# Rotating the order of nine projection units so that two accumulators stay open, with side work placed anew and 32 groups of seven products instead of 33

## The chip, the cores and the metric

The kernel runs on one core of a Trainium2 chip. The metric is the time of the whole program on the device in microseconds (us). TensorE is called PE in the profile, VectorE DVE, ScalarE ACT, GpSimd POOL, and SyncE SP; SP only issues transfers here. Three runs of the kernel before gave 1335.2, 1333.42 and 1333.69 us, with a median of 1333.69 us.

## The reference, cut to what matters

One layer of a diffusion backbone is applied to two groups of 128 tokens (a prompt and a latent grid), model width D = 2048, all in fp32:

```python
sh1, sc1, g1, sh2, sc2, g2 = split(silu(cond) @ w_ada + b_ada)   # per group, w_ada 2048 x 12288
h = rms_norm(x, norm1_w) * (1 + sc1) + sh1
qa, ka, va, qb, kb, vb, ga, gb = split(h @ w_in)                  # w_in 2048 x 8704
oa, ob = window_attention(qa, ka, va), neighbourhood_attention(qb, kb, vb)
x = x + g1 * ((sigmoid(ga) * (oa @ w_br_a) + sigmoid(gb) * (ob @ w_br_b)) @ w_out)
h2 = rms_norm(x, norm2_w) * (1 + sc2) + sh2
x = x + g2 * (square(relu(h2 @ w_up)) @ w_down)                   # 2048 x 8192, 8192 x 2048
```

The outputs are x for both groups and the new keys and values. With only 256 rows of activations, the work is a stream of weights: every weight is read once.

## The kernel before, in words

**Steps.** The weights stream through as 456 steps of one 128x1024 fp32 tile (512 KB, tile `raw`). To keep fp32 accuracy with fp32r products, each tile is split in two: ACT copies it to `wH` (line 93, the helper `copy`), DVE subtracts to get `wL` (line 241), and PE makes three products for each pair of operands: high by high, high by low, low by high. A plain step is 12 matmuls of 128x128 by 128x512. Steps 0 to 71 are the first part (q, k and v of the input projection), 72 to 135 the gates, 136 to 199 the merge and the output projection, 200 to 215 the first eighth of `w_up`. Then `up` and `down` alternate: 16 steps of `w_up` for the next eighth (`up_pair`, L1113), 16 steps of `w_down` for the one before (`down_unit`, L1252), seven times, and 16 steps of `w_down` at the end. Pair 6 is steps 376 to 391, pair 7 steps 408 to 423; behind each come four units of `w_down`, steps 392 to 407 and 424 to 439.

**The first part.** Nine units of 512 columns (`first_units`, L367) are done in five chunks of the inner dimension (`CHUNKS`, 2, 2, 2, 4 and 6 tiles of 128 rows), because the modulation of the rows (`mod_pair`, L415, from pairs of `w_ada` tiles called `araw`, L300, multiplied at L308) is made while it goes on. `start_steps` (L379) runs one unit over one chunk. Each unit has two accumulators of one PSUM bank each; the pool `pacc` has four banks, so two units can be open. At the end of its chunk, a unit is either held open (`hold`, L399) or its two banks are read out: the first time by ACT copies (L403, `first_evac`), afterwards by two DVE adds to the unit's sum in SBUF (L406). Before, the order of units is reversed from chunk to chunk (L433), so the last unit of one chunk is the first of the next, and that one is held.

**Groups of seven.** In `up_pair`, the eight positions of a pair are either plain (two steps, 24 matmuls) or a group of seven products (a step x and a step y, 21 matmuls together, by a recombination of 2x2 blocks). `FAST` lists which positions are groups. A group saves three matmuls, but it needs more of the others: on ACT the copies `XH`, `YB` (half a tile), `tH` and `uH`, on DVE the sum `t` (L1178), three half-tile operations (L1181 to L1183) and the differences `XL`, `tL` and `uL` (L1186 to L1188). `prep_x` issues `XH`; `prep_y` issues all the rest as one block, in the order of the code. A pair opens four banks of `pacc`, Q1, Q6, Q2 and Q7 (L1137), and four of another pool. At position 0 the y step multiplies Q2 first, then Q7, then Q6 (L1123 to L1125).

**The end of a unit of w_down.** `down_unit` adds its two banks to `dsum` on DVE (L1263), except for the units in `SUM_DMA`, where two ACT copies move the banks into a `dsum` part, which a POOL transfer with addition (L1267) adds later. Unit 23 (the fourth unit after pair 6, steps 404 to 407) is one of those.

**Order of the work.** `run` (L264) writes out the program step by step; every engine then works through its own list in that order. For step i it issues loads up to the due time i + `RUN[i]`, then splits (the `prep` functions) up to step i + `LOOK[i]`, then the matmuls of step i with their end, then side work due at i. `LO_DMA` lists steps whose `wL` is made by an ACT pass with sign and a POOL transfer with addition (L247, L248) in place of the DVE operation. All 128x1024 tiles, weights and their halves among them, come from one pool of 48 slots (`GEN`), so a load can wait for a slot. SP issues loads in a single list, in the order written. `DOTS1`, `DOTS`, `DOTS2`, `SS_AT`, `JOBS`, `POST` and the like are due steps of side work (other parts of `w_ada`, attention).

Of the kernel before, what the change touches and what calls it, by code (L numbers as in the profile page):

```python
# [32 lines left out]
FB_DVE = 6  # L33
FB1 = 14
H_AT = 41
DOTS1 = [11, 17, 20, 28, 28, 31, 34, 37]
CHUNKS = [2, 2, 2, 4, 6]
NFAST = 8
FAST = {1: (0, 3, 7), 2: (0, 2, 6, 7), 3: (0, 2, 4, 5, 7), 4: (0, 2, 4, 5, 7), 5: (0, 3, 4, 5, 7), 6: (0, 2, 4, 5, 7), 7: (0, 1, 2, 4, 5, 7)}
SUM_DMA = [5, 6, 11, 13, 16, 19, 21, 23, 25, 27]  # L40
AWAY = [('gA', 1), ('gB', 2), ('gB', 3), ('gA', 0), ('gB', 0), ('gA', 2)]
GATE_BACK = 8
DIRECT = (3,)
LO_DMA = [70, 83, 107, 131, 176, 184, 233, 292, 314, 328, 402, 404]
LO_AHEAD = 2

LOOK = "443323444122344433223333332123333453344534333554455544344534333543324554444555556665556644444333333333332222122312344544555434333333342344333334333323445566643344456656533344434444445455564546555553444554322355444554433333333434334533333333333654544332334455543444555653215536544523333334543233333332223323365455455443222212233432443334434642333334444544534434333333333325434222223333434444444434555642255353443444442222432331122132223342112223332233345544"
RUN = "301110000000010212223333322222222221111122244455544355434445554334554445555664543433234334444445665543321222222212444444444444442222222232223344444455544544444444555455454445566644455555554543365434343355445756644443566664333312222234552332223333334545332333333333322211122222332233322212233323323332332112344444442343322211333343334323233334544422742222212223445554422333233322222211222333333435767545333110221112232111233456655566567556433435335553333334"
CONST_AT = [65, 67]
XL_DMA = []  # L50
ADA_AT = [None, 4, 13, 18, 21, 36, 29]
XS_AT = {1: 13, 2: 18, 3: 29}
POST = {('kvA', 0): [67, 70, 75], ('qA', 0): [70, 73, 78], ('qA', 1): [72, 74, 80], ('kB', 0): [77, 83, 90], ('qB', 0): [82, 84, 93], ('kB', 1): [86, 91, 93], ('qB', 1): [90, 93, 97]}
JOBS = [[79, 80, 80, 87, 93], [81, 83, 88, 90, 93], [87, 87, 89, 90, 99], [93, 93, 96, 99, 102], [96, 97, 100, 105, 112], [102, 103, 107, 112, 123], [105, 107, 111, 118, 123], [112, 115, 118, 121, 123]]
SS_AT = [43, 51, 73, 75, 139, 139]
T_AT = [4, 4]
PREP_IN = [6, 7]
DOTS = [33, 39, 42, 43, 47, 47, 48, 49, 52, 54, 55, 57, 60, 62, 69, 70, 73, 77, 80, 84, 90, 91, 92, 92, 94, 98, 101, 103, 103, 105, 108, 110, 111, 112, 115, 118, 120, 121, 122, 122, 126, 127, 128, 129, 130, 132, 132, 136, 137, 138, 138, 143, 144, 147, 147, 150, 153, 155, 157, 161, 164, 167, 170, 172, 173, 174, 175, 176, 177, 178, 179, 182]
DOTS2 = [230, 232, 234, 235, 236, 237, 240, 243, 255, 263, 265, 269, 270, 288, 301, 301, 307, 328, 328, 331, 333, 334, 358, 360, 361, 363, 366, 368, 391, 391, 395, 399]
STAT_AT = [-1, 0, 10, 16]  # L60
T_PAIR = [[8, 9], [6, 8], [8, 9], [7, 8], [10, 11], [8, 9], [12, 11]]
P_PAIR = [[4, 2], [2, 4], [3, 4], [1, 3], [6, 6], [3, 3], [6, 5]]
M_TE = (3,)
M_AT = [1, 3, 9]
FLIP = 1
P_UP = [4, 1]
T_UP = [6, 5]
COL = {"qA": 0, "kvA": 1024, "qB": 1536, "kB": 2560, "vB": 3584, "gA": 4608, "gB": 6656}


# [1 line left out]
def tile_hybrid_step(ctx: ExitStack, tc: tile.TileContext, a):  # L72
# [188 lines left out]

    by_dma = sorted(LO_DMA)

    def run():  # L264
        loads.sort(key=lambda x: x[:2])
        for st in wsteps:
            while loads and loads[0][0] <= st["i"] + int(RUN[st["i"]]):
                loads.pop(0)[2]()
            for j in sorted(j for j in pre if j <= st["i"]):
                for fn in pre.pop(j):  # L270
                    fn()
            to = st["i"] + int(LOOK[st["i"]]) + 1
            while by_dma and by_dma[0] < to + LO_AHEAD:
# [93 lines left out]
    first_units = [("qA", 0), ("qA", 1), ("kvA", 0), ("qB", 0), ("qB", 1), ("kB", 0), ("kB", 1), ("vB", 0), ("vB", 1)]  # L367
    late_units = []
    nf = len(first_units)
# [9 lines left out]
    def start_steps(u, k0, nk, held, hold):  # L379


        box = {}

        def mm(st, kt):
            if kt == 0:
                box["acc"] = open_acc.pop(u) if held else [bank("acc", pacc) for _ in range(2)]
            acc = box["acc"]
            wh, wl = st["hl"]
            last = kt + 2 == nk
            for k in range(2):  # L390
                g, kg = divmod(k0 + kt + k, 4)
                for tb in range(2):
                    sh, sl = hH[g][:, kg, tb, :], hL[g][:, kg, tb, :]
                    pe.matmul(acc[tb], sh, wh[:, k, :], start=kt == 0 and k == 0 and not held, stop=False)  # L394
                    pe.matmul(acc[tb], sh, wl[:, k, :], start=False, stop=False)  # L395
                    pe.matmul(acc[tb], sl, wh[:, k, :], start=False, stop=last and k == 1 and not hold)  # L396
            if not last:
                return
            if hold:  # L399
                open_acc[u] = acc  # L400
                return
            if u not in units:
                first_evac(u, acc)  # L403
                return
            for tb in range(2):
                dve.tensor_tensor(units[u][:, tb, :], units[u][:, tb, :], acc[tb], op=OP.add)  # L406
            box.clear()

        for kt in range(0, nk, 2):
            add_step(wsrc(w_in, k0 + kt, COL[u[0]] + 512 * u[1]), lambda st, kt=kt: mm(st, kt), u)  # L410
# [4 lines left out]
    def mod_pair(f):  # L415

        box, k0 = {}, 2 * f
        i = ADA_AT[f]
        for j in range(2):
# [9 lines left out]
    for g, i in XS_AT.items():  # L429
        at(i, lambda g=g: x_scale(g))  # L430
    k0 = 0
    for c, nk in enumerate(CHUNKS):
        for j, u in enumerate(first_units[::-1] if c % 2 else first_units):  # L433
            start_steps(u, k0, nk, c > 0 and j == 0, c < len(CHUNKS) - 1 and j == nf - 1)
        k0 += nk

    def begin():
# [108 lines left out]
    def unit_gate(u):  # L546
        def evac(acc):
            gates[u] = G(f"g_{u[0]}{u[1]}").rearrange("p (s n) -> p s n", s=2)
            for tb in range(2):
                act.activation(gates[u][:, tb, :], acc[tb], AF.Sigmoid if u in direct else AF.Copy)  # L550
            if u in AWAY:
                gate_mem[u] = dp.tile([P, 1024], F32, name=f"gm_{u[0]}{u[1]}")
# [62 lines left out]
    s0 = len([st for st in wsteps if st["key"] in first_units])  # L615
    load_at(CONST_AT[0], load_consts)
    load_at(CONST_AT[1], load_bias)

# [58 lines left out]

    for u, ps in POST.items():
        nh = 2 if u[0] == "kvA" else 4
# [99 lines left out]
    att_end = 0  # L779
    for (mix, s, g), js in zip([("A", 0, 0), ("A", 1, 0), ("A", 0, 1), ("A", 1, 1), ("B", 0, 0), ("B", 1, 0), ("B", 0, 1), ("B", 1, 1)], JOBS):  # L780
        need = [POST["kvA", 0][2] + 1, POST["qA", g][2] + 1] if mix == "A" else [
            POST["kB", g][2] + 1, POST["qB", g][2] + 1, end_of(("vB", g)) + 1]
        assert js[0] >= max(need) and list(js) == sorted(js)
# [8 lines left out]
    def sigmoids():  # L792
        for u in gates:
            if u not in direct and u not in AWAY:
                sigmoid(u)
# [93 lines left out]
    for n in range(4):  # L889
        br_unit(n)  # L890
    for u in AWAY:
        i = end_of(("y" + u[0][1].lower(), u[1]))
        load_at(i - GATE_BACK, lambda u=u: gate_back(u))
        at(i - 2, lambda u=u: sigmoid(u))
# [81 lines left out]
    def norm2(s):  # L976
# [3 lines left out]
        rsqrt(r, ms, EPS)  # L980
        prep_to(end_of(("out", 3)) + 1 + PREP_IN[s])
        for n in range(4):
# [130 lines left out]
    def up_pair(p):  # L1113
        n0, n1 = PIECES[p]
        w, box, key = a["w_up"], {"begun": set()}, ("up", n0)
        fast = FAST[p]

# [134 lines left out]
    def down_unit(p, n):  # L1252
        def evac(acc):
            by_pool = 4 * p + n in SUM_DMA
            if p == 0 or by_pool:
# [24 lines left out]
    for n in range(4):  # L1280
        at(end_of(("up", 0)) + 1 + n, lambda n=n: x1_away(n))
    for g in range((max(len(f) for f in FAST.values()) + 1) // 2):
        at(end_of(("up", 0)) + STAT_AT[g], lambda g=g: fast_stat(g))
    for p in range(len(PIECES)):
        if p < last and p + 1 not in FAST:
            for n in PIECES[p + 1]:
# [92 lines left out]
    jobs1 = [((0, w), fb) for fb in range(FB1, KC) for w in range(2)]  # L1379
    first = list(zip(DOTS1, [(j, 0, 0) for j in jobs1] + [(j, 1, 1) for j in jobs1], strict=True))  # L1380
    placed = list(zip(DOTS, [(j, 1, 0) for j in g1 + ss] + [(j, 0, 1) for j in g1 + ss], strict=True))
    assert DOTS[-1] < end_of(("out", 2))
# [12 lines left out]
    for c in range(FB_DVE // 2):  # L1395
        box = {}
        for j in range(2):
            i = SS_AT[2 * c + j]
            load_at(i, lambda box=box, c=c, j=j: pair_load(box, 1, 2 * c + j))
# [104 lines left out]
```

## The time and the profile before, and how to read them

| | |
|---|---|
| median of three runs | 1333.69 us (1333.42 to 1335.2) |
| the profiled execution's own time | 1333.2 us |
| its span | 1331.4 us, mean granted TensorE clock 0.998 |
| traffic | 392.24 MB, mean 295 GB/s |

The profiled execution's time is 1.8 us above its span, for what lies around the span. All positions in time are counted in us from the span's start. The profile gives each engine's busy time, windows of time with each engine's busy time and instruction counts, groups of like instructions with the mean time of one, the waits of an engine with what ended them, the timeline of single instructions, and a chain of waits followed back from the last instruction. In a window, the number in brackets behind a busy time counts the instructions that lie in it, also in part; PEclk is the clock granted to TensorE as a share of full speed. Matmuls are pipelined: one shows some 390 ns, but the next one starts earlier, so it is the distance from start to start that tells PE's pace.

### The profile page before, as it was taken

To read this page: it belongs to the slowest core of one execution; us is meant where nothing else is said; L and a number is where in the kernel's file an instruction comes from. 1 tells how busy PE (TensorE), PEld (TensorE's weight loads), DVE (VectorE), ACT (ScalarE), POOL (GpSimd) and SP (SyncE) were. 2 spreads that over 40 slices of the span, in tenths; PEclk is the share of its full clock that TensorE was granted. 3 is DMA by queue.
4 is the path that set the end of the run, shared out by engine and by line. 5 is a ranking of instruction groups with operands and counts; after the bars stand their busy time and mean duration, and the time that the engine had idled before them with its cause. 6 is when DMAs were issued, how large, how long until landed. Compare 5 with 4: busy or idle time off the path is not lost.

```text
span 1331.4 us, 18029 instructions
## 1 busy us (share of the span) xinstructions
PE 1316.4 (99%) x6411; PEld 1067.2 (80%) x6412; DVE 1185.6 (89%) x1538; ACT 801.2 (60%) x979; POOL 54.0 (4%) x64
## 2 busy tenths in 40 slices
PE   8999999999999999999999999999999999999998
PEld 4777778788888878888888888888888888877887
DVE  4589999988898999999779998998999999989685
ACT  5534443476656446635677866758576576676670
POOL 0000000521000000000000000000000000000000
PEclk9999999999999999999999999999999999999999
DMA  9999998987589999996577876988797696988962
GB/s 372 408 409 408 409 398 303 383 277 240 182 326 354 383 394 352 362 359 218 191 225 279 285 252 214 290 278 264 237 298 252 237 300 206 313 192 296 329 210 98
DMA packets 148266, 392.24 MB, mean 295 GB/s; under 512 B 51792, under 2 KB 53008, under 8 KB 148176
## 3 DMA queue, kind: packets, MB, share of 16 engines
q1 hardware_dynamic: 144448, 378.16, 78.9%
q0 software_dynamic: 3584, 12.85, 5.0%
q8 instruction: 50, 0.82, 0.2%
q14 instruction: 40, 0.33, 0.1%
q10 hardware_dynamic: 144, 0.08, 0.0%
HBM read 367.16 MB, written 8.68 MB: 282 GB/s over the span
## 4 chain that ended last, share of the span: by engine, by line
PE 93%; DMA 4%; ACT 1%; DVE 1%; issue 0%; SPq 0%; DVEq 0%; ACTq 0%
PE acc L291 17%; PE acc L292 17%; PE acc L293 17%; PE Q L1123 6%; PE Q L1124 6%; PE Q L1125 6%; PE acc L394 4%; PE acc L395 4%; PE acc L396 4%; DMA araw<-in_w_pair 3%; PE ps_ada L308 2%; PE ps_S L713 1%; PE Z L1124 1%; PE Z L1123 1%; PE Z L1125 1%; DMA aT<-in_w_adaT 1%
## 5 line engine op out<-in xcount | busy, mean ns | idle before, releaser
L241 DVE TENSOR_TENSOR wL<-raw,wH 128x1024 fp32r<-128x1024 f32 x375 | 446.6, 1224 | 72.2 <-ACT wH L93 67.9
L93 ACT ACTIVATE wH<-raw 128x1024 fp32r<-128x1024 f32 (+1 forms) x393 | 393.0, 1044 | 128.2 <-PE acc L395 22.5
L394 PE MATMUL acc<-wH,hH 128*128 128x512 f32 x276 | 109.0, 395 | 0.0
L396 PE MATMUL acc<-wH,hL 128*128 128x512 f32 x276 | 107.5, 390 | 0.0
L395 PE MATMUL acc<-wL,hH 128*128 128x512 f32 x276 | 107.5, 389 | 0.0
L291 PE MATMUL acc<-wH,hH 128*128 128x512 f32 x256 | 101.4, 396 | 0.0
L293 PE MATMUL acc<-wH,hL 128*128 128x512 f32 x256 | 99.7, 390 | 0.0
L292 PE MATMUL acc<-wL,hH 128*128 128x512 f32 x256 | 99.7, 390 | 0.0
L1333 DVE CUSTOM_DVE_ANT_0 aT<-aT,cB,cols 128x1024 f32<-128x1024 f32 x56 | 71.7, 1285 | 0.2
L1333 DVE CUSTOM_DVE_ANT_0 junk<-aT,cB,cols 128x1024 bf16<-128x1024 f32 x56 | 71.4, 1280 | 0.0
L93 ACT ACTIVATE tH<-t 128x1024 fp32r<-128x1024 f32 x33 | 35.0, 1061 | 57.7 <-DVE t L1178 55.0
L394 PEld LDWEIGHTS acc<-wH,hH 128*128 128x128 f32 x276 | 51.8, 188 | 13.5 <-issue 2.9
L396 PEld LDWEIGHTS acc<-wH,hL 128*128 128x128 f32 x276 | 51.8, 188 | 11.0
L395 PEld LDWEIGHTS acc<-wL,hH 128*128 128x128 f32 x276 | 51.9, 188 | 10.4
L293 PEld LDWEIGHTS acc<-wH,hL 128*128 128x128 f32 x256 | 48.1, 188 | 10.2
L291 PEld LDWEIGHTS acc<-wH,hH 128*128 128x128 f32 x256 | 48.1, 188 | 9.8 <-ACT sq L628 0.4
L292 PEld LDWEIGHTS acc<-wL,hH 128*128 128x128 f32 x256 | 48.1, 188 | 9.3
L93 ACT ACTIVATE uH<-raw 128x1024 fp32r<-128x1024 f32 x33 | 35.1, 1062 | 32.0 <-DVE raw L1183 27.7
L1229 ACT ACTIVATE up<-up 128x1024 f32<-128x1024 f32 x28 | 29.7, 1062 | 26.8 <-DVE up L1223 26.4
L308 PE MATMUL ps_ada<-araw,cpad 128*32 128x256 f32 x640 | 39.1, 382 | 2.9 <-DMA araw<-in_w_pair 2.7
L93 ACT ACTIVATE fTa<-pTa 128x2048 uint16<-128x2048 uint16 x16 | 40.5, 2534 | 2.0 <-PE acc L292 1.4
L1178 DVE TENSOR_TENSOR t<-raw 128x1024 f32<-128x1024 f32 x33 | 40.2, 1220 | 1.0 <-PE acc L292 1.0
(641 smaller groups left out, 3311.1 us busy)
## 6 DMA issues: line engine op xcount, KB each, us to landing
raw<-in_w_in SPq DMA_DIRECT2D x133, 512.0 KB, 9.1
raw<-in_w_down SPq DMA_DIRECT2D x128, 512.0 KB, 5.7
araw<-in_w_pair SPq DMA_DIRECT2D x80, 512.0 KB, 10.2
raw<-in_w_upF SPq DMA_DIRECT2D x66, 512.0 KB, 5.1
aT<-in_w_gT SPq DMA_DIRECT2D x64, 512.0 KB, 7.2
raw<-in_w_up SPq DMA_DIRECT2D x62, 512.0 KB, 5.2
aT<-in_w_adaT SPq DMA_DIRECT2D x48, 512.0 KB, 9.6
raw<-in_w_out SPq DMA_DIRECT2D x32, 512.0 KB, 9.7
```

The source lines that it names most:

```text
L93: act.activation(out, in_, AF.Copy)
L241: dve.tensor_tensor(st["lo"], st["raw"], st["hi"].bitcast(F32), op=OP.subtract)
L291: pe.matmul(acc[tb], sh, wh[:, k, :], start=f, stop=False)
L292: pe.matmul(acc[tb], sh, wl[:, k, :], start=False, stop=False)
L293: pe.matmul(acc[tb], sl, wh[:, k, :], start=False, stop=l)
L394: pe.matmul(acc[tb], sh, wh[:, k, :], start=kt == 0 and k == 0 and not held, stop=False)
L395: pe.matmul(acc[tb], sh, wl[:, k, :], start=False, stop=False)
L396: pe.matmul(acc[tb], sl, wh[:, k, :], start=False, stop=last and k == 1 and not hold)
L1123: pe.matmul(acc, stat[0], hi, start=f, stop=False)
L1124: pe.matmul(acc, stat[0], lo, start=False, stop=False)
L1125: pe.matmul(acc, stat[1], hi, start=False, stop=l)
L1333: dve.tensor_tensor_reduce(out, box["raw"], cB[s, tag], 1.0, dst if second else baT[:, part, fb:fb + 1], OP.mult, OP.add, dst)
```

## The change

Five things change, all in the order and placement of work; no function is new.

1. **The order of units in the first part.** Each chunk starts with the last two units of the chunk before, in the same order, and both are held open over the change. The last change before the final chunk is arranged so that the final chunk runs in the plain order. The chunks' orders become 0..8; 7, 8, 0..6; 5..8, 0..4; 3..8, 2, 0, 1; 0..8 (units by their place in `first_units`).
2. **`FAST`**: pair 2 has its groups at positions 0, 4, 5, 7 (before 0, 2, 6, 7), pair 6 at 0, 2, 5, 6, 7 (before 0, 2, 4, 5, 7), and pair 7 at 0, 1, 3, 5, 7 (before 0, 1, 2, 4, 5, 7). That is 32 groups in place of 33.
3. **`SUM_DMA`** loses unit 27, **`LO_DMA`** loses steps 70, 83, 328 and 402 and gains 89 and 319.
4. **`LOOK` and `RUN`** change at some hundred steps, mostly by one. At the end of pair 6's `w_down`, `LOOK` goes from 3, 5, 3, 3, 4 to 2, 4, 2, 3, 3 at steps 405 to 409.
5. **Due steps of side work**: among them the pair of `w_ada` tiles number 3 from step 18 to 16 and number 6 from 29 to 32 (`ADA_AT`), two of `SS_AT`, entries of `DOTS1`, `DOTS` and `DOTS2`; one gate less is parked in memory (`AWAY`).

The diff, with the two long digit strings and some of the due times left out:

```diff
-DOTS1 = [11, 17, 20, 28, 28, 31, 34, 37]
+DOTS1 = [11, 15, 27, 29, 29, 30, 32, 35]
-FAST = {1: (0, 3, 7), 2: (0, 2, 6, 7), 3: (0, 2, 4, 5, 7), 4: (0, 2, 4, 5, 7), 5: (0, 3, 4, 5, 7), 6: (0, 2, 4, 5, 7), 7: (0, 1, 2, 4, 5, 7)}
-SUM_DMA = [5, 6, 11, 13, 16, 19, 21, 23, 25, 27]
-AWAY = [('gA', 1), ('gB', 2), ('gB', 3), ('gA', 0), ('gB', 0), ('gA', 2)]
-GATE_BACK = 8
+FAST = {1: (0, 3, 7), 2: (0, 4, 5, 7), 3: (0, 2, 4, 5, 7), 4: (0, 2, 4, 5, 7), 5: (0, 3, 4, 5, 7), 6: (0, 2, 5, 6, 7), 7: (0, 1, 3, 5, 7)}
+SUM_DMA = [5, 6, 11, 13, 16, 19, 21, 23, 25]
+AWAY = [('gB', 2), ('gA', 0), ('gB', 0), ('gA', 2), ('gB', 3)]
+GATE_BACK = 6
-LO_DMA = [70, 83, 107, 131, 176, 184, 233, 292, 314, 328, 402, 404]
+LO_DMA = [89, 107, 131, 176, 184, 233, 292, 314, 319, 404]
...
-ADA_AT = [None, 4, 13, 18, 21, 36, 29]
+ADA_AT = [None, 4, 13, 16, 21, 36, 32]
...
-SS_AT = [43, 51, 73, 75, 139, 139]
+SS_AT = [41, 57, 73, 75, 135, 139]
...
     k0 = 0
+    order, ends = list(first_units), len(CHUNKS) - 1
     for c, nk in enumerate(CHUNKS):
-        for j, u in enumerate(first_units[::-1] if c % 2 else first_units):
-            start_steps(u, k0, nk, c > 0 and j == 0, c < len(CHUNKS) - 1 and j == nf - 1)
+        if c == ends - 1:
+            order = [u for u in order if u not in first_units[:2]] + first_units[:2]
+        if c == ends:
+            order = first_units
+        for j, u in enumerate(order):
+            start_steps(u, k0, nk, c > 0 and j < 2, c < ends and j >= nf - 2)
+        order = order[-2:] + order[:-2]
         k0 += nk
```

More of the change, by code (lines that the diff above doesn't have):

```diff
@@ L43 @@
+SUM_DMA = [5, 6, 11, 13, 16, 19, 21, 23, 25]
+AWAY = [('gB', 2), ('gA', 0), ('gB', 0), ('gA', 2), ('gB', 3)]
+GATE_BACK = 6
 DIRECT = (3,)
-LO_DMA = [70, 83, 107, 131, 176, 184, 233, 292, 314, 328, 402, 404]
+LO_DMA = [89, 107, 131, 176, 184, 233, 292, 314, 319, 404]
 LO_AHEAD = 2
-LOOK = "443323444122344433223333332123333453344534333554455544344534333543324554444555556665556644444333333333332222122312344544555434333333342344333334333323445566643344456656533344434444445455564546555553444554322355444554433333333434334533333333333654544332334455543444555653215536544523333334543233333332223323365455455443222212233432443334434642333334444544534434333333333325434222223333434444444434555642255353443444442222432331122132223342112223332233345544"
@@ L48 @@
-RUN = "301110000000010212223333322222222221111122244455544355434445554334554445555664543433234334444445665543321222222212444444444444442222222232223344444455544544444444555455454445566644455555554543365434343355445756644443566664333312222234552332223333334545332333333333322211122222332233322212233323323332332112344444442343322211333343334323233334544422742222212223445554422333233322222211222333333435767545333110221112232111233456655566567556433435335553333334"
-CONST_AT = [65, 67]
+LOOK = "652422234122454433223333332123333453344534333554455544344534333543324554444555556665556644444333333333332222122312344544555434333333342344333334333323445566643344456656433344434444445455564546555553444554322466554554433333333434334533333333333654544332334455643444555653315536554523333334543233333332223323365455455443222212233432443334434642333334444544534434333333333325434222223333434444444434555642255242433444442233554442233242223342112224442233345544"
@@ L50 @@
+RUN = "300000000000010212223333322222222221111122244455544355434445554334554445555775654544345434444445665543321222222212444444444444442222222232223344444455544544444444555454454466677755566555554543365434343355445756644443566664333312222234552332223333334545332333333333322211133333332233311101234434433332332112444444442454322211333343334323233334544422742222212223445554422333233322222211222333333435767445344121210002232000233455555566567556433435335553333334"
+CONST_AT = [67, 70]
 XL_DMA = []
-ADA_AT = [None, 4, 13, 18, 21, 36, 29]
+ADA_AT = [None, 4, 13, 16, 21, 36, 32]
@@ L52 @@
 XS_AT = {1: 13, 2: 18, 3: 29}
-POST = {('kvA', 0): [67, 70, 75], ('qA', 0): [70, 73, 78], ('qA', 1): [72, 74, 80], ('kB', 0): [77, 83, 90], ('qB', 0): [82, 84, 93], ('kB', 1): [86, 91, 93], ('qB', 1): [90, 93, 97]}
-JOBS = [[79, 80, 80, 87, 93], [81, 83, 88, 90, 93], [87, 87, 89, 90, 99], [93, 93, 96, 99, 102], [96, 97, 100, 105, 112], [102, 103, 107, 112, 123], [105, 107, 111, 118, 123], [112, 115, 118, 121, 123]]
-SS_AT = [43, 51, 73, 75, 139, 139]
+POST = {('kvA', 0): [67, 70, 75], ('qA', 0): [70, 73, 78], ('qA', 1): [72, 74, 80], ('kB', 0): [77, 86, 90], ('qB', 0): [82, 84, 93], ('kB', 1): [87, 92, 95], ('qB', 1): [90, 93, 96]}
@@ L56 @@
+JOBS = [[79, 80, 80, 87, 93], [81, 83, 88, 90, 93], [87, 87, 89, 90, 96], [93, 93, 96, 102, 105], [96, 97, 100, 105, 112], [102, 103, 107, 112, 123], [105, 107, 111, 118, 123], [112, 115, 118, 121, 123]]
+SS_AT = [41, 57, 73, 75, 135, 139]
 T_AT = [4, 4]
-PREP_IN = [6, 7]
-DOTS = [33, 39, 42, 43, 47, 47, 48, 49, 52, 54, 55, 57, 60, 62, 69, 70, 73, 77, 80, 84, 90, 91, 92, 92, 94, 98, 101, 103, 103, 105, 108, 110, 111, 112, 115, 118, 120, 121, 122, 122, 126, 127, 128, 129, 130, 132, 132, 136, 137, 138, 138, 143, 144, 147, 147, 150, 153, 155, 157, 161, 164, 167, 170, 172, 173, 174, 175, 176, 177, 178, 179, 182]
@@ L59 @@
[L59 to L62, printed above, removed]
+PREP_IN = [6, 4]
+DOTS = [33, 39, 42, 45, 47, 48, 49, 50, 53, 55, 55, 55, 60, 65, 69, 70, 73, 75, 80, 84, 90, 91, 92, 93, 95, 100, 101, 103, 103, 104, 108, 110, 111, 112, 115, 118, 120, 122, 123, 124, 126, 127, 128, 129, 130, 132, 133, 134, 137, 138, 138, 143, 144, 145, 147, 150, 153, 157, 159, 160, 166, 167, 170, 172, 173, 174, 175, 176, 178, 178, 179, 183]
@@ L63 @@
+DOTS2 = [230, 232, 234, 235, 236, 237, 240, 243, 255, 263, 265, 269, 270, 288, 300, 300, 306, 328, 328, 331, 333, 334, 358, 360, 362, 364, 368, 368, 391, 391, 395, 399]
+STAT_AT = [-1, 0, 10, 11]
+T_PAIR = [[10, 8], [6, 8], [8, 10], [5, 7], [10, 13], [8, 9], [12, 11]]
+P_PAIR = [[5, 2], [2, 4], [3, 5], [-1, 3], [5, 8], [3, 3], [7, 4]]
 M_TE = (3,)
-M_AT = [1, 3, 9]
+M_AT = [1, 3, 8]
 FLIP = 1
-P_UP = [4, 1]
-T_UP = [6, 5]
+P_UP = [2, 2]
+T_UP = [7, 5]
 COL = {"qA": 0, "kvA": 1024, "qB": 1536, "kB": 2560, "vB": 3584, "gA": 4608, "gB": 6656}
```

## The prediction, as put on record before the run

> **What bounds the kernel now.** I read the page first, its busy times and the chain that ended last, then the waits of PE.
>
> ```profile
> PE 1316.4 (99%) x6411; PEld 1067.2 (80%) x6412; DVE 1185.6 (89%) x1538; ACT 801.2 (60%) x979; POOL 54.0 (4%) x64
> PE 93%; DMA 4%; ACT 1%; DVE 1%; issue 0%; SPq 0%; DVEq 0%; ACTq 0%
> ```
>
> ```profile
> PE Q L1123 <- ACT dsum L93: 3.6, 1, 3.6
> PE ps_ada L308 <- DMA araw<-in_w_pair: 2.7, 5, 0.6
> PE acc L467 <- ACT hH L93: 1.3, 2, 0.9
> ```
>
> PE carries 93% of the chain, and its three longest waits come to 7.6 us. DVE is at 89%, so it could become the bound anywhere, but it is not the bound now. A busy share can mislead with pipelined matmuls, so I read the pace from windows.
>
> ```profile
> 100.00:150.00 50.00, 50.00 (x332) 38.55 (x324) 47.85 (x72) 21.05 (x25) 0.00 (x0) 1.00 1.03 409
> 950.00:1000.00 50.00, 50.00 (x222) 41.42 (x221) 47.82 (x56) 35.35 (x39) 0.86 (x1) 1.00 0.82 275
> 1190.00:1200.00 10.00, 6.40 (x28) 4.99 (x28) 9.90 (x12) 5.99 (x9) 0.00 (x0) 1.00 0.52 161
> 1200.00:1210.00 10.00, 10.00 (x38) 8.05 (x37) 9.93 (x12) 6.76 (x8) 0.87 (x1) 0.83 0.89 256
> 1210.00:1220.00 10.00, 10.00 (x46) 8.29 (x45) 9.86 (x13) 5.03 (x7) 0.00 (x0) 1.00 0.86 312
> ```
>
> In an ordinary stretch (950 to 1000) 222 matmuls touch 50 us: 0.226 us each from start to start, the pace of a PE that waits for nothing; a plain step of 12 takes 2.72 us. The first part (100 to 150) is harder to read, since short matmuls raise its count, but PE is busy all through while DMA is full (1.03, 409 GB/s) and DVE is at 47.85 of 50. So **no time is lost there that a lighter DVE could return**. One place stands out: 1190 to 1210 holds 28 and 38 matmuls where 46 are usual, so 26 are missing, 5.9 us with one or two edge counts in it. The timelines of PE, ACT and DVE there:
>
> ```profile
> 1194.12 0.39 PE L293 MATMUL acc<-wH,a11L 128*128 128x512 f32 x1
> ...
> 1195.25 0.39 PE L1124 MATMUL Q<-YB,h20H 128*128 128x512 f32 x1
> 1195.48 0.39 PE L1125 MATMUL Q<-YB,h20L 128*128 128x512 f32 x1
> 1199.46 0.50 PE L1123 MATMUL Q<-tH,sH 128*128 128x512 f32 x1 [3.60 <-ACT dsum L93]
> ...
> 1200.88 0.63 PE L1125 MATMUL Q<-uH,sL 128*128 128x512 f32 x1
> 1201.31 0.63 PE L1123 MATMUL Q<-tH,sH 128*128 128x512 f32 x1
> ```
>
> ```profile
> 1191.27 1.06 ACT L93 ACTIVATE uH<-raw 128x1024 fp32r<-128x1024 f32 x1 [1.00 <-DVE raw L1183]
> ...
> 1193.18 0.61 ACT L93 ACTIVATE YB<-raw 128x512 fp32r<-128x512 f32 x1
> 1195.81 1.06 ACT L93 ACTIVATE tH<-t 128x1024 fp32r<-128x1024 f32 x1 [2.02 <-DVE t L1178]
> 1197.87 1.06 ACT L93 ACTIVATE uH<-raw 128x1024 fp32r<-128x1024 f32 x1 [1.00 <-DVE raw L1183]
> 1198.83 1.07 ACT L93 ACTIVATE dsum<-acc 128x512 f32<-128x512 f32 x2
> ```
>
> ```profile
> 1194.50 1.22 DVE L1178 TENSOR_TENSOR t<-raw 128x1024 f32<-128x1024 f32 x1
> ...
> 1197.08 0.69 DVE L1183 TENSOR_TENSOR raw<-raw 128x512 f32<-128x512 f32 x1
> 1197.69 1.22 DVE L1186 TENSOR_TENSOR XL<-raw,XH 128x1024 fp32r<-128x1024 f32 x1
> 1198.83 1.22 DVE L1187 TENSOR_TENSOR tL<-t,tH 128x1024 fp32r<-128x1024 f32 x1
> 1199.96 1.22 DVE L1188 TENSOR_TENSOR uL<-raw,uH 128x1024 fp32r<-128x1024 f32 x1
> ```
>
> This is the start of pair 7. Q7 needs a bank that unit 23 has just filled. Unit 23 is read out by ACT (`dsum`), and its last matmul started at 1194.12. But ACT's list has the second group's YB (1193.18), tH and uH ahead of the copies; tH waits for DVE's t, uH for raw at 1197.77. The copies start at 1198.83 and Q7 at 1199.46, not at 1195.48 + 0.23 = 1195.71: **3.75 us lost**. Then the clock falls (0.83 over the window) and matmuls start 0.43 us apart for about 8 of them: 8 x (0.43 − 0.226) = **1.6 us**. Two windows check this sum, each a pair with its units of w_down:
>
> ```profile
> 1110.40:1194.30 83.90, 83.90 (x371) 69.21 (x370) 75.70 (x86) 59.39 (x63) 3.47 (x4) 1.00 0.80 240
> 1194.30:1282.80 88.50, 84.90 (x367) 69.78 (x367) 72.38 (x79) 54.97 (x57) 1.73 (x2) 0.98 0.98 315
> ```
>
> Pair 6 (five groups) takes 83.9 us, pair 7 (six groups, so three matmuls or 0.68 us less work) 88.5 us: 88.5 − 83.9 + 0.68 = 5.3 us of loss, against 3.75 + 1.6 = 5.35.
>
> **The change part by part.** Prices of DVE's work, from its groups:
>
> ```profile
> L241 DVE TENSOR_TENSOR wL<-raw,wH 128x1024 fp32r<-128x1024 f32 x375 | 446.6, 1224 | 72.2 <-ACT wH L93 67.9 <-DMA aT<-in_w_gT 3.2 <-issue 0.6
> L1181 DVE TENSOR_TENSOR raw<-t,raw 128x512 f32<-128x512 f32 x33 | 22.8, 692 | 1.1
> L1263 DVE TENSOR_TENSOR dsum<-dsum,acc 128x512 f32<-128x512 f32 x28 | 18.2, 682 | 2.7 <-PE acc L293 2.7
> L406 DVE TENSOR_TENSOR u_qB<-u_qB,acc 128x512 f32<-128x512 f32 x16 | 10.2, 682 | 0.0
> ```
>
> *Two units held.* Of the 64 adds at L406, 8 go: 8 x 0.68 = 5.5 us of DVE. They lie in the first part, where PE waits for no DVE. Two open units fill all four banks at a change of chunk, but the third unit of a chunk needs the banks of the first one, which has a whole step (2.72 us) for its two adds (1.36 us); that is the same alternation as before. PE: 0. The adds buy DVE room, which is then spent: four steps leave `LO_DMA` and two join, 2 x 1.22 = +2.4 us, and unit 27's adds return, +1.4 us.
>
> *Groups.* One group fewer: three matmuls more on PE, 3 x 0.226 = **+0.68 us**. On DVE a group has four full operations and three half ones, 4 x 1.22 + 3 x 0.69 = 6.95 us, a plain position 2 x 1.22 = 2.45 us: −4.5 us. In sum DVE has −5.5 + 2.4 + 1.4 − 4.5 = −6.2 us.
>
> *Pair 7 and `LOOK`.* After unit 23's last step, splits now reach one step less far: ACT's order is the first group, XH of the second, the two `dsum` copies, and only then YB, tH, uH. The copies start when PE ends the unit, about 1194.5, and end at 1195.6. Q7 is due at 1195.7 and Q6, with the other bank, at 1196.4. **The 3.75 us go, and the half clock with them, −1.6 us.** What is late next: YB is behind the copies, 1195.6 to 1196.2, and DVE's YB operation wants it at 1196.36, so DVE keeps its beat by 0.15 us. XL of the second group ends at 1198.9. Without the stall, position 0 takes 21 matmuls, 4.77 us, from 1194.35 to 1199.1, and XL is read one matmul later, at 1199.35: **0.4 us to spare**. tL ends at 1200.05 for a use at about 1201.2, uL at 1201.2 for 1202.7. Position 2 is now plain, so DVE gains on PE there (2.45 us of DVE for 5.45 us of PE), where before came a third group (6.95 for 4.77). I take 0 for a new stall; the other end is 0.8, if the beat slips by one 1.22 operation (1.22 − 0.4). Step 402's wL, now on DVE just ahead of this, is such an operation: it lies in DVE's idle time (7.53 of 10 us busy in the row below).
>
> ```profile
> 1180.00:1190.00 10.00, 10.00 (x46) 8.29 (x45) 7.53 (x9) 7.39 (x7) 0.00 (x0) 1.00 0.67 201
> ```
>
> *Side work.* The pair of w_ada tiles number 3 moves from step 18 to 16. Before:
>
> ```profile
> 67.25 7.69 SPq L300 DMA_DIRECT2D araw<-in_w_pair  x8
> 85.05 3.66 PE L308 MATMUL ps_ada<-araw,cpad 128*32 128x256 f32 x64
> DMA to landing us min/median/max: 8.6/10.2/10.2
> ```
>
> Its last load is issued at 67.25 + 7.69 − 0.33 = 74.6 and lands 10.2 later, 84.8; its last eighth of work starts at 85.05 + 7/8 x 3.66 = 88.25: 3.4 us to spare. After, work starts after step 16, two steps earlier (85.05 − 5.44 = 79.6), its last eighth at 82.8. The loads stand two places earlier in SP's list, and with DMA full a place is 512 KB / 409 GB/s = 1.28 us: 82.25. **About half a microsecond to spare**, so 0; the other end is a rival. Number 6 moves later, toward more room. The rest (other `LOOK` and `RUN` entries, dots, parking one gate less) I cost at 0: they lie on ACT (60%), DVE and DMA beside a PE that waits for none of them now; the bound below is −1.4, if the remaining short waits went (the w_pair ones, 2.7 us in all, half of them), and above +1.2, one DVE operation come late.
>
> *Sum.* −3.75 − 1.6 + 0.68 = −4.67. The profiled execution took 1333.2 (span 1331.4 and 1.8 around it): 1328.5. It lies 0.5 below the median 1333.69, so as a median **1329.0 us**.
>
> The half clock began after 3.75 us of idle and lasted about 3.4 us. The Trainium skill, page "TensorE: Matmul & The Clock Gate", section "Part 1: The HAM clock gate (the "warmup" mystery)", says that the clock halves after an idle window of about 3.4 us, that the window is free-running, and that a busy window restores it. The row agrees in size. By that rule an idle time so little over one window need not halve the clock in every execution; the sum would then be −3.75 + 0.68 = −3.1, which is the last rival below.
>
> **The rivals.**
>
> *A wait of DVE takes its place.* The second group's XL is late by up to 0.8 us, and pair 6, which now has three groups in a row at its end, loses some: each group costs DVE 6.95 − 4.77 = 2.2 us of its lead. For it: DVE is at 9.9 of 10 in three windows above. Against: DVE has 6.2 us less to do. 0.8 in pair 7 and as much again, up to 2.2, in pair 6: 1329.8 to 1332.
>
> *It doesn't do what it says.* The copies stay late, for instance because the first group's uH, ahead of them, waits for DVE; holding accumulators brings nothing by itself. Then 1333.69 + 0.68 = 1334.4. Against: that uH ran in time before, at 1191.27.
>
> *Slower: a load of the first part misses its use.* SP issues in one list, and a load that waits for a slot holds all behind it:
>
> ```profile
> SPq L215 <- DVE wL L241: 43.8, 26, 6.8
> ```
>
> ```profile
> GB/s 372 408 409 408 409 398 303 383 277 240 182 326 354 383 394 352 362 359 218 191 225 279 285 252 214 290 278 264 237 298 252 237 300 206 313 192 296 329 210 98
> ```
>
> The longest such wait is 6.8 us. DMA is full from 33 to 167 us (the page's slices of 33.3 us, the second to the fifth), so a hold is not made up. If one comes ahead of pair 3 at step 16, PE waits 6.8 − 0.5 = 6.3 us and runs another 1.6 us' worth at half clock: 1329.0 + 7.9 = 1336.9. It decides from 0.5 us of slip, and the kernel is slower than before from 4.7 us of such loss in all. Against: the transfers here flow without a gap, with 8 loads in flight (10.2 / 1.28), which covers a hold shorter than 10 us.
>
> *Only the wait goes.* If other executions of before did not fall to half clock, their median never held those 1.6 us, and the median falls by 3.1 only: 1330.6. Against: the three runs lie at 1333.4 and above, none of them 1.6 below the profiled 1333.2.
>
> **How the numbers follow.** My forecast of 1329.0 has 0.66, a DVE wait 0.12, only the wait 0.03, no effect 0.09, slower 0.10. A measurement of this kernel can tell about 0.2% from no change, 2.7 us: 1331.0 and 1336.4 are the borders. Faster: 0.66 + 0.03 and half of 0.12, 0.75. Within: the other half and 0.09, 0.15. Slower: 0.10. The range reaches from 1327.4 (short waits gone too) up over the DVE wait to no effect, 1334.5, and leaves out the slow case.
>
> **What would show it.** In the profile after, the wait of Q at L1123 for ACT `dsum` is gone or below 0.5 us; the windows from pair 7's start hold 45 or 46 matmuls for 10 us at clock 1.00; the stretch from pair 7's first matmul to the end of its units takes about 84 us, like pair 6; L406 shows 56 adds and no wait of PE moves in the first part. Wrong would be a wait of PE at L1124 for XL or tL in pair 7, a wait at L308 of over 1 us near 80 us, or a clock below 1.00 anywhere past the start. If the time falls much below 1327, something in the first part was lost that I read as hidden.

## The result and the profile after

| | before | after |
|---|---|---|
| median | 1333.6 us (1332.54 to 1335.41, 6 runs) | 1329.26 us (1328.93 to 1330.41, 6 runs) |
| profiled execution, span | 1333.2, 1331.4 us | 1329.24, 1327.5 us |

The ratio is 0.9968, with a 95% interval of 0.9956 to 0.998: 4.3 us faster, against a forecast of 1329.0 us.

The first four waits of PE after, longest in all first (each line: PE's tile and line, what it waited for, us in total, times, longest):

```profile
PE ps_ada L308 <- DMA araw<-in_w_pair: 2.5, 5, 0.6
PE acc L473 <- ACT hH L93: 1.3, 2, 0.9
PE ps_warm L117 <- DVE wm L110: 1.2, 1, 1.2
PE ps_gr L1352 <- DVE gc_g L1339: 1.0, 1, 1.0
```

The 3.6 us of Q7 are gone, and one line is new: ps_gr waits 1.0 us for DVE. It is PE's transpose of the second gate's columns (`gate_rows`), which needs the last dot products of DVE (`gc_g`). The windows of pair 6 with its four units, of pair 7 with its units, and the three 10-us windows around the start of pair 7 (PE, PEld, DVE, ACT, POOL busy, clock, DMA share, GB/s):

```profile
1110.40:1195.30 84.90, 83.94 (x371) 69.18 (x371) 77.64 (x88) 58.38 (x62) 2.58 (x3) 1.00 0.82 250
1195.30:1279.00 83.70, 83.70 (x371) 69.28 (x370) 67.56 (x74) 59.04 (x62) 1.72 (x2) 1.00 0.94 308
1190.00:1200.00 10.00, 10.00 (x46) 8.29 (x45) 9.86 (x12) 6.97 (x9) 0.86 (x1) 1.00 0.54 146
1200.00:1210.00 10.00, 10.00 (x46) 8.28 (x45) 9.93 (x11) 6.63 (x9) 0.00 (x0) 1.00 0.98 328
1210.00:1220.00 10.00, 10.00 (x46) 8.29 (x45) 9.93 (x11) 6.67 (x9) 0.00 (x0) 1.00 0.83 259
```

Each of the three 10-us windows holds 46 matmuls at full clock, where before the first two held 28 and 38. Pair 7's stretch falls from 88.5 to 83.7 us, −4.8; pair 6's rises from 83.9 to 84.9, +1.0 by the new wait. That is −3.8, and the two spans differ by −3.9: in these two executions, the rest of the program keeps its time within 0.1 us in sum. ACT's and PE's timelines at the same place:

```profile
1192.46 1.04 ACT L93 ACTIVATE XH<-raw 128x1024 fp32r<-128x1024 f32 x1
1194.88 1.28 ACT L93 ACTIVATE dsum<-acc 128x512 f32<-128x512 f32 x2 [1.37 <-PE acc L293]
1196.05 0.62 ACT L93 ACTIVATE YB<-raw 128x512 fp32r<-128x512 f32 x1
```

```profile
1196.49 0.39 PE L1131 MATMUL Q<-YB,h20L 128*128 128x512 f32 x1
1196.72 0.39 PE L1129 MATMUL Q<-tH,sH 128*128 128x512 f32 x1
```

The `dsum` copies now stand ahead of YB and wait only for PE's own end of the unit (1.37 us of ACT idle, which costs nothing). Q7 starts 0.23 us after Q2's last matmul: at pace. (Behind the first part, lines after are 6 higher: L1123 is now L1129.)

### The profile page after: what moved, and what is told of

Read it like the earlier page. It is cut to its first block, busy times and chain, and to the rows that moved or that the text cites. A ratio compares the mean times of both kernels' runs of the same rounds, so it can differ in the third digit from the quotient of the medians.

```text
span 1327.5 us, 18042 instructions
## 1 busy us (share of the span) xinstructions
PE 1314.7 (99%) x6414; PEld 1066.7 (80%) x6415; DVE 1179.5 (89%) x1529; ACT 796.3 (60%) x973; POOL 49.9 (4%) x61
## 4 chain that ended last, share of the span: by engine, by line
PE 94%; DMA 4%; DVE 1%; ACT 0%; POOL 0%; issue 0%; SPq 0%; ACTq 0%
PE acc L291 17%; PE acc L293 17%; PE acc L292 17%; PE Q L1129 6%; PE Q L1131 6%; PE Q L1130 6%; PE acc L394 4%; PE acc L395 4%; PE acc L396 4%; DMA araw<-in_w_pair 3%; PE ps_ada L308 2%; DMA raw<-in_w_in 1%; PE Z L1129 1%; PE Z L1131 1%; PE Z L1130 1%; PE ps_S L719 1%
## 5 line engine op out<-in xcount | busy, mean ns | idle before, releaser
L308 PE MATMUL ps_ada<-araw,cpad 128*32 128x256 f32 x640 | 39.3, 382 | 2.6 <-DMA araw<-in_w_pair 2.5
```

## The experiments

My theory after the result: the gain is the order of ACT's list at the end of unit 23 and one group less right behind it; the new order of the first part brings nothing; and 1.0 us is lost again at ps_gr. The rivals: the lighter DVE brings the gain (6.2 us less work, of which the held units are 5.5), or the held units themselves do. Eleven kernels were run in three sets, each beside the kernel before, whose median was 1333.08, 1332.91 and 1332.93 us (the first four kernels of the table, the next four, the last three).

| kernel | median us | ratio to before, 95% interval |
|---|---|---|
| look_alone | 1330.89 | 0.9977 to 0.9995 |
| hold_alone | 1332.73 | 0.9989 to 1.0007 |
| old_look | 1333.77 | 1.0000 to 1.0018 |
| rows_later | 1327.79 | 0.9954 to 0.9979 |
| look_fast7 | 1328.16 | 0.9950 to 0.9977 |
| pair3_at15 | 1331.29 | 0.9979 to 0.9996 |
| lo402 | 1328.14 | 0.9952 to 0.9977 |
| best | 1329.31 | 0.9962 to 0.9983 |
| after_old_loop | 1329.05 | 0.9959 to 0.9981 |
| fast7_alone | 1333.11 | 0.9995 to 1.0013 |
| rows_ss | 1327.68 | 0.9948 to 0.9973 |

The intervals are against the kernel before. A step of 1 us or so between two of the new kernels rests on their medians, and on a trace that shows the wait behind it.

### Five entries of LOOK alone, on the kernel before

The fourth of the five is the same in both.

```diff
 # LOOK at steps 405 to 409
-3, 5, 3, 3, 4
+2, 4, 2, 3, 3
```

> The kernel before with only five entries of LOOK changed (steps 405 to 409 as in the changed kernel); pair 7 keeps its six groups, the first part its one held unit. Theory (the gain is ACT's order at the end of unit 23): the wait of Q7 for the dsum copies and the half clock go, 5.35 us, but the third group in a row finds DVE late: its XL would end near 1205.5 and be wanted at 1204.1 to 1204.3, so 1.2 to 1.4 us come back as a wait at L1124. 1333.6 - 5.35 + 1.3 = 1329.6. Rival (the gain needs the lighter DVE of fewer groups and adds): the late third group eats most of it, 1332 or more. Rival (held accumulators bring it): 1333.6, nothing.

1330.89 us, 2.2 us faster, where 1329.6 was expected. Its waits of PE, two of its lines:

```profile
PE Q L1124 <- DVE XL L1186: 1.5, 2, 1.3
PE acc L292 <- DVE wL L241: 0.5, 1, 0.5
```

No line of Q for ACT's `dsum` is left: the order of the copies alone removes that wait. But three groups in a row now run into DVE, as PE's and DVE's timelines show for the third one:

```profile
1204.80 0.39 PE L1123 MATMUL Q<-XH,h21H 128*128 128x512 f32 x1
1206.49 0.50 PE L1124 MATMUL Q<-XL,h21H 128*128 128x512 f32 x1 [1.30 <-DVE XL L1186]
```

```profile
1205.22 1.22 DVE L1186 TENSOR_TENSOR XL<-raw,XH 128x1024 fp32r<-128x1024 f32 x1
```

XL ends at 1206.44, and its matmul, due at 1205.03, starts at 1206.49: 1.46 us late. PE waits 0.2 us more for XL in a later group of the pair (at 1222 us, the second of the two waits) and 0.5 us for a wL at 1246 us. So the waits of DVE were real without FAST's change: some 2 us where 1.2 to 1.4 were expected. The rest of the miss against 1329.6 is not placed. The profiled execution was the slowest of the eleven (1331.82 us), since it holds a stretch at half clock elsewhere, around 43 us. Its windows 38 to 42 and 42 to 46, and the second one in the kernel before:

```profile
38.00:42.00 4.00, 2.30 (x25) 0.55 (x25) 0.00 (x0) 0.00 (x0) 0.00 (x0) 0.89 1.03 409
42.00:46.00 4.00, 4.00 (x13) 3.17 (x14) 2.36 (x2) 3.00 (x4) 0.00 (x0) 0.69 1.03 410
```

```profile
42.00:46.00 4.00, 4.00 (x22) 3.31 (x21) 2.34 (x3) 3.92 (x6) 0.00 (x0) 1.00 1.03 411
```

In both kernels PE waits three times for some 0.6 us just before, for loads of a pair of `w_ada` tiles; the clock fell in one execution and not in the other.

### Pair 7's groups alone, on the kernel before

```diff
-FAST[7] = (0, 1, 2, 4, 5, 7)
+FAST[7] = (0, 1, 3, 5, 7)
```

> The kernel before with pair 7's groups at 0, 1, 3, 5, 7 and nothing else. Theory (the wait of Q7 is made by ACT's order alone): the wait stays at 3.6 us and three matmuls more cost 0.68 us: 1333.0 + 0.68 = 1333.7. Rival (fewer groups in a row relieve DVE and so shorten the wait): below 1331.

1333.11 us, no change. Its first wait of PE:

```profile
PE Q L1123 <- ACT dsum L93: 3.6, 1, 3.6
```

The wait is there to the tenth: with `LOOK` as it was, a lighter DVE behind the place does not shorten it. The expected 0.68 us more lies inside the interval (−0.7 to +1.7 us) and is not told apart from nothing.

### Both together, on the kernel before

The two edits above in one kernel, and nothing else.

> The kernel before with the five entries of LOOK at steps 405 to 409 and pair 7's groups at 0, 1, 3, 5, 7 as in the changed kernel; nothing else, so the first part holds one unit and step 402's wL stays with POOL. Theory (these two edits are the whole gain): the wait of Q7 goes, the 1.5 us wait for XL of the third group that LOOK alone left goes too, and the wait of ps_gr does not come: 1333.1 - 5.35 + 0.68 = 1328.4, under the changed kernel's 1329.3. Rival (the 6 us that DVE saves elsewhere are needed, or the held accumulators carry part of the gain): 1330 or more.

1328.16 us: two edits give 4.75 us by the medians, at least as much as the whole change. Forecast was 1328.4. No wait of PE for DVE's XL is left: in the second group of pair 7, XL ends 0.42 us ahead of its matmul, and the prediction had 0.4. One wait of the old kind stands in its trace, at the start of another pair (944 us):

```profile
PE Q L1123 <- ACT dsum L93: 0.8, 1, 0.8
```

Up to that place its program is that of the kernel before and of `look_alone`, and their traces do not have this wait. So waits of this size come and go from one execution to another.

### The old LOOK, in the changed kernel

```diff
 # LOOK at steps 405 to 409 of the changed kernel
-2, 4, 2, 3, 3
+3, 5, 3, 3, 4
```

> The changed kernel with LOOK at steps 405 to 409 as before. Theory: the copies stand behind YB, tH and uH of the second group again, so Q7 waits 3.7 us and the clock falls to half for 3.4 us: 1329.3 + 5.3 = 1334.6. Rival (plain position 2 and a lighter DVE remove the wait by themselves): 1329.3 to 1330.

1333.77 us, 4.5 us slower than the changed kernel; all of the gain is lost. ACT's timeline and PE's:

```profile
1197.50 1.06 ACT L93 ACTIVATE uH<-raw 128x1024 fp32r<-128x1024 f32 x1 [0.93 <-DVE raw L1189]
1198.47 1.07 ACT L93 ACTIVATE dsum<-acc 128x512 f32<-128x512 f32 x2
```

```profile
1195.98 0.39 PE L1131 MATMUL Q<-YB,h20L 128*128 128x512 f32 x1
1199.10 0.50 PE L1129 MATMUL Q<-tH,sH 128*128 128x512 f32 x1 [2.73 <-ACT dsum L93]
...
1200.63 0.63 PE L1131 MATMUL Q<-uH,sL 128*128 128x512 f32 x1
1201.06 0.63 PE L1129 MATMUL Q<-tH,sH 128*128 128x512 f32 x1
```

The copies are behind uH again. The wait is 2.73 us and not 3.6. That fits the new wait of ps_gr, which delays PE and not DVE's chain to uH: Q2's last matmul starts 0.50 us later than before, and the copies start 0.36 us earlier. Of two delays on different engines only the later counts. The half clock (0.43 us from start to start) came all the same. In this trace Q7 starts 2.9 us late, and the next twelve starts take 4.45 us in place of 2.72, 1.7 us more: 4.6 us in all, against 4.5 between the medians.

### The held units: alone, and taken out

The first kernel is the one before with the new loop of the first part; the second is the changed kernel with the old loop. In the diff, the first kernel reads from minus to plus, the second from plus to minus.

```diff
-        for j, u in enumerate(first_units[::-1] if c % 2 else first_units):
-            start_steps(u, k0, nk, c > 0 and j == 0, c < len(CHUNKS) - 1 and j == nf - 1)
+        if c == ends - 1:
+            order = [u for u in order if u not in first_units[:2]] + first_units[:2]
...
+        for j, u in enumerate(order):
+            start_steps(u, k0, nk, c > 0 and j < 2, c < ends and j >= nf - 2)
+        order = order[-2:] + order[:-2]
```

> The kernel before with only the new order of the first part, two units held, 56 adds at L406 in place of 64; every due step as before. Theory: PE waits for no DVE there, so 1333.6 with at most 0.7 either way, and the wait of Q7 stands as before. Rival (held accumulators bring the gain through 5.5 us less of DVE): 1329 to 1331.

> The changed kernel with the old order of the first part: one unit held, 64 adds at L406 in place of 56, every due step as changed. Theory (DVE is so nearly full between 100 and 250 us that the 5.5 us of adds are what pays for steps 70 and 83 coming back to DVE and for side work placed earlier, though they bring nothing by themselves): waits of PE for DVE (L406 or wL) between 100 and 350 us, some 1 to 3 us in all, 1330.3 to 1332.5. Rival (the adds lie beside PE without effect, as forecast): 1329.3.

1332.73 us (no change, and its trace has the 3.6 us wait of Q7 as before) and 1329.05 us (the changed kernel has 1329.26). For the second I had expected waits of DVE, since the first part is so full; **that theory fell**. The windows 100 to 150, 150 to 200 and 200 to 250 of the changed kernel, then of the changed kernel with the old loop:

```profile
100.00:150.00 50.00, 50.00 (x328) 38.50 (x320) 45.76 (x67) 20.41 (x24) 0.00 (x0) 1.00 1.03 409
150.00:200.00 50.00, 49.72 (x253) 39.91 (x250) 48.29 (x74) 22.20 (x27) 0.00 (x0) 1.00 1.01 394
200.00:250.00 50.00, 50.00 (x247) 40.56 (x246) 47.56 (x71) 19.52 (x21) 7.35 (x8) 1.00 0.84 324
```

```profile
100.00:150.00 50.00, 50.00 (x336) 38.72 (x328) 46.94 (x70) 20.29 (x24) 0.00 (x0) 1.00 1.03 408
150.00:200.00 50.00, 50.00 (x273) 39.93 (x266) 49.89 (x76) 21.84 (x26) 0.00 (x0) 1.00 0.99 387
200.00:250.00 50.00, 50.00 (x247) 40.51 (x247) 47.84 (x72) 19.09 (x21) 6.85 (x7) 1.00 0.85 324
```

DVE carries 3.1 us more in these 150 us (144.67 against 141.61) and reaches 49.89 of 50, and still no wait of PE for it appears in the first part. The new order of the units, which the title names first, has no effect on the time that these runs can tell (`hold_alone`: −1.5 to +0.9 us).

### The new wait of ps_gr: two ways to take it away

Once the transposes come one step later, once step 402's wL goes back to ACT and POOL.

```diff
-    ex(i, lambda: gate_rows("g2"))
+    ex(i + 1, lambda: gate_rows("g2"))
```

```diff
-LO_DMA = [89, 107, 131, 176, 184, 233, 292, 314, 319, 404]
+LO_DMA = [89, 107, 131, 176, 184, 233, 292, 314, 319, 402, 404]
```

> The changed kernel with the transposes of the second gate's columns (ps_gr) one step later, after step 402 in place of 401. Theory: the new wait of 1.0 us of ps_gr for DVE gc_g goes, since the dots end at 1178.9 and the next step ends at 1180.6: 1329.3 - 1.0 = 1328.3. Rival (the wait only moves, to the planes or to XL of pair 7's second group, which has 0.4 us to spare): 1329.3.

> The changed kernel with step 402 back among the steps whose wL is made by ACT and POOL. Theory (this one DVE operation, ahead of the last dots in DVE's list, made ps_gr wait): the wait of 1.0 us goes, 1329.3 - 1.0 = 1328.3, as with the transposes one step later (1327.8). Rival (the wait comes of LOOK at 399 to 401 or of pair 6's groups): the wait stays, 1329.3.

1327.79 and 1328.14 us, with 1328.3 expected of both. Both rid the trace of the wait. The chain of waits of the changed kernel shows what made it:

```profile
1175.07 1.23 DVE wL L241
1176.30 1.20 DVE junk L1339
...
1178.74 0.10 DVE gc_g L1339
1178.84 0.04 issue
1178.88 0.28 PE ps_gr L1352
```

A wL is in DVE's list ahead of the last two dots (`junk` is the first), and PE's transposes need the dots. DVE stands idle for 1.04 us just ahead of that wL; for what, the profile does not say. With step 402 off DVE, `lo402`, the dots end 1.2 us earlier:

```profile
1175.05 1.28 DVE L1339 CUSTOM_DVE_ANT_0 junk<-aT,cB,gc_g 128x1024 bf16<-128x1024 f32 x1
...
1177.59 0.09 DVE L1339 DVE_READ_ACCUMULATOR2_ANT gc_g<- 128x1 f32 x1
```

### A load's margin: the pair of w_ada number 3 one step earlier

```diff
-ADA_AT = [None, 4, 13, 16, 21, 36, 32]
+ADA_AT = [None, 4, 13, 15, 21, 36, 32]
```

> The changed kernel with the w_ada pair number 3 due at step 15 in place of 16. In the changed kernel's trace the last of its eight loads lands 0.6 us ahead of its use. Its work comes one step earlier (2.72 us), its loads one place earlier in SP's list (1.28 us). Theory (the place in the list sets the landing, DMA being full): a wait of 2.72 - 1.28 - 0.6 = 0.85 us at L308 near 77 to 80 us, so 1329.3 + 0.85 = 1330.1. Rival (the loads have room, as the transfers in flight cover it): 1329.3.

1331.29 us, 2.0 us slower than the changed kernel, where 0.85 was expected. The work on the last of the eight loads, in PE's timeline:

```profile
76.49 3.58 PE L308 MATMUL ps_ada<-araw,cpad 128*32 128x256 f32 x56
80.73 0.64 PE L308 MATMUL ps_ada<-araw,cpad 128*32 128x256 f32 x8 [0.66 <-DMA araw<-in_w_pair]
```

PE waits 0.66 us for the last load, so the place in SP's list does set the landing, and step 16 was as near to a stall as the margin said. Two more waits of PE stand in this trace:

```profile
PE Q L1129 <- DVE dsum L1269: 0.4, 1, 0.4
PE acc L396 <- DVE hL L97: 0.3, 1, 0.3
```

Counted by how late the matmuls start against pace, the three are 1.0 (the load), 0.5 (dsum, at 862 us) and 0.5 us (hL, at 89 us), 2.0 in all. That is as much as the medians differ; the two profiled spans differ by 2.6. So the forecast missed what stands behind the load's wait. That the edit made the wait for dsum, 780 us later, is not shown. `look_alone`, which leaves `ADA_AT` alone, has the same wait at 861 us, and the kernel before, whose program is the same up to there, has not:

```profile
PE Q L1123 <- DVE dsum L1263: 0.3, 1, 0.3
```

### Taking small waits away

`best` has the later transposes, the fifth of `SS_AT` back from 135 to 139, and pair 5 of w_ada at step 37; `rows_ss` is the same with pair 5 at 36.

```diff
-ADA_AT = [None, 4, 13, 16, 21, 36, 32]
+ADA_AT = [None, 4, 13, 16, 21, 37, 32]
...
-SS_AT = [41, 57, 73, 75, 135, 139]
+SS_AT = [41, 57, 73, 75, 139, 139]
```

> The changed kernel with the transposes of the gate's columns one step later (1327.8 measured), the fifth of SS_AT back from 135 to 139 (one change between tile shapes on PE less, 0.30 us), and the w_ada pair number 5 at step 37 in place of 36, whose last load lands 0.65 us late: its use comes 2.72 us later, its loads one place (1.28 us). Theory: 1327.8 - 0.30 - 0.65 = 1326.9. Rival (a small wait gained back only lets PE run into the next late operand, since DVE is nearly full there): 1327.8.

> The changed kernel with the transposes of the gate's columns one step later and the fifth of SS_AT back at 139; pair 5 stays at step 36. Theory (the 1.9 us wait for the adds of u_kB came from pair 5 at step 37 alone): that wait is gone and one change of tile shape less saves 0.30 us: 1327.8 - 0.3 = 1327.5. Rival (the two products at step 139, whose loads now come four steps later, hold PE): 1328 or more.

`best` gives 1329.31 us, 1.5 us worse than with the later transposes alone. Both its theory (1326.9) and its rival (1327.8) missed; the rival named the right kind of cause. Its wait, in PE's timeline:

```profile
147.44 0.39 PE L396 MATMUL acc<-wH,hL 128*128 128x512 f32 x1
149.58 0.47 PE L394 MATMUL acc<-wH,hH 128*128 128x512 f32 x1 [1.75 <-DVE u_kB L406]
```

Pair 5's products had held PE for some 3.7 us just there. Without them PE arrives at step 38 before DVE has emptied the banks that were filled two steps earlier. `rows_ss` has no such wait: 1327.68 us, as expected (1327.5). It is the fastest of all, 5.2 us under the kernel before, but its step from `rows_later` (0.1 us) is less than the runs can tell.

## Why the prediction was right, point by point

- **The wait of Q7 (−3.75) and the half clock (−1.6).** Right in place, cause and size. `look_alone` shows that these entries of `LOOK`, and with them ACT's order, remove the wait by themselves; `old_look` shows that they bring it back.
- **One group less (+0.68) and plain position 2.** Right as a pair: without it 2 us of DVE waits come back (`look_alone`), with it none. The term −4.67 is met by `look_fast7`, which has just these edits: −4.75 by the medians, with an interval of −6.7 to −3.1. The +0.68 by itself is not told apart from nothing (`fast7_alone`).
- **Two units held: 0.** Right, from both sides: `hold_alone` and `after_old_loop`.
- **Step 402's wL: "it lies in DVE's idle time".** This step failed. In DVE's list it stands ahead of the last dots, which start at 1176 us, and so ahead of the window 1180 to 1190 that was read for it. The idle time of that window lay behind the last dots, and PE's transposes wait for the dots, not for DVE's next weight. Costed 0, measured 1.0 us. It was my upper bound for one late operation (+1.2), at another place than I had named.
- **Side work: 0, with half a microsecond to spare at step 16.** Right: the margin holds, and one step more breaks it (`pair3_at15`). The other edits of this kind, and the groups of pairs 2 and 6, were not run alone. What lies between `look_fast7` and the changed kernel is 1.1 us by the medians, of which ps_gr has 1.0.
- **The sum.** −4.67 + 1.0 = −3.67; the profiled executions differ by −3.96 and the medians by −4.3. The remaining 0.3 us, and what the medians give beyond it, is not traced to one place. The 0.5 us by which the forecast went from the profiled execution to the median did not come again: after, the two are 1329.24 and 1329.26. So part of the match with 1329.0 is luck: the miss at ps_gr (+1.0) is offset by these two.
- **"Only the wait goes".** This rival did not come true. All four traces with the long wait show the half clock behind it (the kernel before, `old_look`, `fast7_alone` and `hold_alone`), and the medians of `old_look` and the changed kernel differ by 4.5 us, the wait and the half clock together. In how many other executions the clock fell is open. In the 61 runs of the kernel before beside the experiments, the mean granted clock is 0.999 in six, which took 1330.81 to 1331.58 us, and 0.996 to 0.998 in the others, from 1331.90 up. One stretch of 3.4 us at half clock lowers the mean by 0.0013, so the six would fit one stretch fewer, 1.6 us. But a mean does not tell where the clock fell: the trace of `fast7_alone` has the stretch behind Q7 at a mean of 0.999, and others fall around 43 us or at the very end, when PE has no more work. The Trainium skill ("TensorE: Matmul & The Clock Gate", section "Part 1: The HAM clock gate (the "warmup" mystery)") has the window free-running, so that a short idle time may or may not fill one. These runs agree with it in so far as the same waits around 40 us were followed by half clock in three of the thirteen traces. They do not agree with the size, an idle window of about 3.4 us, that the prediction quotes from there: in `old_look` the clock fell after a wait of 2.73 us, and around 40 us after three waits of 0.6 us. The measurement decides.

## What to carry to other kernels

A bank's release is an instruction in an engine's list like any other: look at what stands ahead of it, above all at splits prepared early that wait for a third engine, and move the release ahead of them before lightening any engine. A mean busy share says little about an edit: here 5.5 us of DVE work fewer at 97% busy gave nothing, and one operation of 1.2 us, put ahead of the wrong neighbour on an engine with idle time left, cost 1.0 us. When a wait is taken away, the next operand must be shown to be in time; here a plain position behind two groups was what made it so.

## What the runs showed of the hardware

- The clock fell to half after a wait of 2.73 us (`old_look`), less than the 3.6 us of the kernel before. Waits of 1.0 us (ps_gr) and 1.75 us (`best`) at full pace around them were not followed by it. Three waits of some 0.6 us each within 4 us, with only the small matmuls of L308 between them, were followed by it in three of thirteen traces (`look_alone`, `after_old_loop`, `best`) and not in the other ten.
- A change of PE from the small tile shape (128x256 outputs on 32 columns) to full 128x128 matmuls shows 0.2 to 0.3 us more than pace at ten places of the kernel before's trace. An example follows: twelve small matmuls start 0.054 us apart (64 of them take 3.66 us and 8 take 0.64), so the full one was due at 88.53 and starts at 88.64, and the next one follows after 0.34 us in place of 0.227.

```profile
87.88 0.83 PE L308 MATMUL ps_ada<-araw,cpad 128*32 128x256 f32 x12
88.64 0.50 PE L394 MATMUL acc<-wH,hH 128*128 128x512 f32 x1
88.98 0.40 PE L395 MATMUL acc<-wL,hH 128*128 128x512 f32 x1
```
